# A modulation third taken off TensorE, its sums in halves, and the pieces loaded from GpSimd's queue

## The chip, the cores and the metric

The kernel runs on one core of a Trainium2 chip. The metric is the device time of one execution in microseconds. The profile shows the core's engines: PE is TensorE, DVE is VectorE, ACT is ScalarE, POOL is GpSimd, SP is SyncE, which here only issues DMA transfers.

## The reference

Two layers of a network over 256 latent and 256 context tokens of width 1024, in float32. Each layer is a token mixer (a long convolution, a gated linear recurrence called RG-LRU, a second recurrence called HGRN2, joined by gates: the merge) and an MLP, and each of the two is wrapped in norms that are scaled, shifted and gated by a modulation:

```python
for layer in range(DEPTH):
    ada_lat = silu(c) @ w_ada[layer] + b_ada[layer]          # 1024 -> 6 * 1024
    ada_ctx = silu(c_ctx) @ w_ada[layer] + b_ada[layer]
    sh1, sc1, g1, sh2, sc2, g2 = split(ada_lat, 6)            # the same for ctx
    u = rmsnorm(h, gains[0]) * (1 + sc1) + sh1
    m = mixer(u)
    h = h + g1 * rmsnorm(m, gains[1])
    f = square(relu((rmsnorm(h, gains[2]) * (1 + sc2) + sh2) @ w_mlp1[layer])) @ w_mlp2[layer]
    h = h + g2 * rmsnorm(f, gains[3])
```

Layer 1 needs no context output, so only its first two chunks (sh1, sc1) are needed for the context. The modulation is a product of two rows (latent and context) with a 1024 x 6144 matrix per layer: little arithmetic, 24 MB of weights. The long convolution also needs a filter per layer, a small network of sines.

## The kernel before

The program is unrolled, and a scheduler orders each engine's instructions by written order, priorities and readiness. The large products are split in high and low halves (three products for one). A weight unit of 1 MB arrives in one of two `raw` buffers, ScalarE writes its high half `wh`, VectorE subtracts to the low half `wl`, and TensorE uses both. A step of the loops below is one such unit, in most places 48 products of 512 columns.

Side work is written as generators and put into a queue `bg`; each loop step calls `bg.step()` once, which writes out the next piece of the first generator in the queue (a class `Pump`). The steps: one for each two column blocks of the projections (L1328), two for each gate branch of the merge beside its four gate steps (L1538), one for each of the 16 blocks of the first MLP product (L1648), one for each of 14 units of the second (L1660). At the end of layer 0's merge (L1540) and before layer 1's first norm (L1663) the queue is drained.

A third of a modulation, numbered s, is 2048 columns (two chunks) of one layer. The first third of layer 0 is computed at the start from a rearranged copy. The others are done in two ways:

- `ada_steps` (L382), for third 1 of layer 0: eight 1 MB pieces go through the `raw` buffers, and on each TensorE forms four narrow products (32 columns of weights `cst`, 512 columns of piece) that stand side by side in the array. Here and in `ada_sums` the two rows end in PSUM.
- `ada_sums` (L429), for the others: pieces of 128 x 512 arrive in four buffers `AM` by DMA from SP's queue, one transfer each, and VectorE multiplies each by a column of `cst` and adds it to a running sum `t` (one sum for each row and column block). A plan is four pieces; eight plans make a third. When a half is done (`both`, two rows) or a third (one row), four narrow products with a 0/1 column `sel` bring the sums over the partitions to PSUM. The first of them is tied behind the products that TensorE had at that step. The `AM` buffers hold the attention scores of the second recurrence at other times, and are zeroed on GpSimd afterwards.

`ada_out` copies the rows out, transposes them to columns (four transposes), adds the bias, and for thirds 1 and 2 multiplies the gate chunk by the norm's gains and stores it in DRAM, from where it is loaded as broadcast rows.

Order before: third 1 of layer 0 in the first projections of layer 0, third 2 of layer 0 for both rows in its merge, the three thirds of layer 1 in the MLP, then the filters of layer 1, in four groups, in the last steps of the second MLP product. The filters take their buffers from the 14 temporaries `t`, as do the sums.

In layer 1 the gates of the RG-LRU (`lru_gates`) are three products each, and those of the first channel block are tied behind 24 products that are written later (`tie(ins, 24)`).

Of the kernel before, what the change touches and what calls it, by code (L numbers as in the profile page):

```python
# [96 lines left out]
def prepare(inp):  # L97
# [11 lines left out]
    for w in range(2):  # L109
        for n in range(2):  # L110
            c = (w + 1) * 2048 + (2 * w + n) * 512
            for l in range(2):
                for r in range(2):
                    o = 32 * (2 * n + r) + w if (l, w) == (0, 1) else 32 * (2 * w + n) + r
# [12 lines left out]
    for l in range(2):  # L127
        for name, val in (("gain0", g["norm_gains"][l, 0]), ("gain2", g["norm_gains"][l, 2]), ("sw", g["hy_short_w"][l]),
# [3 lines left out]
            c = channel_cols(val)  # L132
# [30 lines left out]
def _body(ctx, tc, I, out, cfg):  # L163
# [100 lines left out]
    def add(o, a, b):  # L264
        tt(o, a, b, ALU.add)
# [67 lines left out]

    cst = kt([128, 8, 32])
    pool.memset(cst, 0.0)
    sel = kt([128, 2, 32])
    pool.memset(sel, 0.0)
    for r in range(2):
        pool.memset(sel[:, r, r:r + 1], 1.0)
    csg = kt([128, 8, 2])  # L340
    sigmoid()
    fn(csg, cc, AF.Sigmoid)
# [36 lines left out]
        mul(a0[:, ::-1, ks], part[:, :, 0], col(0, "gain0", 2 * qr, 2)[:, None, :].to_broadcast([128, 2, 2]))  # L379
        yield  # L380

    def ada_steps(l, s):  # L382
        acc = psx('a')
        for k in range(8):
            raw = raw_tile()
            dma(raw, I["w_ada"][l, k * 128:k * 128 + 128, s * 2048:s * 2048 + 2048])
            with tc.high_priority(cfg["AP"]):
                for j in range(4):
                    mm(acc[32 * j:32 * j + 32, :], cst[:, k, :], raw[:, j * 512:j * 512 + 512], k == 0, k == 7,
                       tile_position=(0, 32 * j))  # L390
            yield
        ada_out(l, s, acc, "(j r)")
        yield

    def ada_out(l, s, acc, order):

        rows = tmp()
        dve.tensor_copy(rows, acc)
        pt = psx('a')
        for b in range(4):  # L400
            pe.transpose(pt[:, b * 128:b * 128 + 128], rows[:, b * 128:b * 128 + 128], ident)
        cols = kt([128, 2, 2, 8], name="ac")
        if order == "(j r)":
            pv = pt.rearrange("p (b m n r) -> p r m n b", b=4, m=2, n=2)
        else:
            pv = pt.rearrange("p (b n r m) -> p r m n b", b=4, n=2, r=2)[:, :, :2]
        for r in range(2):
            for m in range(2):
                add(cols[:, r, m].rearrange("p (n b) -> p n b", b=4), pv[:, r, m],
                    col(l, "ba", 16 * s + 8 * m, 8).rearrange("p (n b) -> p n b", b=4))  # L410
        ada_cols[l, s] = cols
        if s > 0:
            w, j0 = s - 1, 2 * (s - 1)
            gr, br = tmp(), tmp()
            dma(gr, I["gate_rows"][l, w, :, 0])
            dma(br, I["gate_rows"][l, w, :, 1])
            add(rows, rows, br)
            mul(gr, gr, rows)
            st = dr.tile([2, 2, 512], F32, name=nm("gd"))
            for n in range(2):  # L420
                if order == "(j r)":
                    dma(st[:, n, :], gr[32 * (j0 + n):32 * (j0 + n) + 2, :])
                    continue
                for r in range(2):
                    o = 32 * (2 * n + r) + w
                    dma(st[r:r + 1, n, :], gr[o:o + 1, :])
            G_rows[l, w] = st

    def ada_sums(l, thirds):  # L429

        plans = [(s, both, i) for s, both in thirds for i in range(8)]

        def pieces(s, both, i):

            if not both:
                return [(i, s * 2048 + n * 512, n) for n in range(4)]
            half, kk = divmod(i, 4)
            return [(2 * kk + a, s * 2048 + half * 1024 + n * 512, n) for a in range(2) for n in range(2)]  # L440

        def load(q, plan):
            k, c, _ = pieces(*plan)[q]
            dma(AM[q], I["w_ada"][l, k * 128:k * 128 + 128, c:c + 512])

        def rows(acc, w, src, start, stop):
            for j, g in enumerate((3, 0, 1, 2)):
                after = last_mm[0]
                with tc.high_priority(cfg["AP"]):
                    ins = mm(acc[32 * g:32 * g + 32, :], w, src(g), start, stop, tile_position=(0, 32 * g))  # L450
                if j == 0:
                    tc.add_manual_dep(ins, after.name, no_sync, reason="behind the products of this step")

        for q in range(4):
            load(q, plans[0])
        acc, due = None, []
        for at_, (s, both, i) in enumerate(plans):
            yield
            while due:
                due.pop(0)()  # L460
            if i == 0 or (both and i == 4):
                sums = {}
            for q, (k, _, n) in enumerate(pieces(s, both, i)):
                for r in range(1 + both):
# [9 lines left out]
            def reduce(s=s, both=both, i=i, sums=sums):  # L474
                nonlocal acc
                if i == 3 or not both:
                    acc = psx('a')
                if both:
                    rows(acc, sel[:, i // 4, :], lambda g: sums[g % 2, g // 2], i == 3, i == 7)
                else:  # L480
                    rows(acc, sel[:, 0, :], lambda g: sums[0, g], True, True)
                if i == 7:
                    ada_out(l, s, acc, "(n r m)" if both else "(j r)")
            if i == 7 or (both and i == 3):
                due.append(reduce)
        yield
        while due:
            due.pop(0)()
        for a_t in AM:
            pool.memset(a_t, 0.0)  # L490
        yield

    def modulation(l, which):

        a, b = kt([128, 2, 8], name="ma"), kt([128, 2, 8], name="mb")
        gain = ("gain0", "gain2")[which]
        for r in range(2):
# [437 lines left out]
    def lru_gates(l, d, c, x, bd, sp_pos):  # L935
# [14 lines left out]
        for g, o in ((0, r), (1, i)):  # L950
            p = psx('l')
            cs = slice(c * 128, c * 128 + 128)
            if l == 1:
                ins = mm(p, bd[d][g][0][:, cs], hi, True, False)
                mm(p, bd[d][g][0][:, cs], lo, False, False)
                mm(p, bd[d][g][1][:, cs], hi, False, True)
                if c == 0:
                    tie(ins, 24)
            else:
                mm(p, bd[d][g][:, cs], xc, True, True)  # L960
            fn(o, p, AF.Sigmoid, bias=col(l, ("br", "bi")[g], d * 4 + c))
# [319 lines left out]
    def layer(l, S, xs=None, es=None):  # L1281
# [220 lines left out]
        for bi, b in enumerate(cfg["ORD"][l]):  # L1502
            Yb = ysplit(b)
            gates = raw_cols((GATES + b * 1024) // 128, 8, not full)
            if not gone:
                side.until("hg", done)
                sigmoid()
                gone = True
                if l == 0:
                    bg.put(ada_sums(0, ((2, True),)))  # L1510
            for x in gates:
                fn(x, x, AF.Sigmoid)
            if bi == 2:
# [112 lines left out]
        for r in range(0 if full else 2, 16):  # L1626
# [12 lines left out]
            for p in ps:  # L1639
# [206 lines left out]
```

## Time and profile before

| | us |
|---|---|
| median of 3 runs (1486.86 to 1488.83) | 1488.61 |
| the profiled execution | 1483.6 |
| its span | 1481.8 |
| TensorE busy in the span | 1454.7 |
| VectorE busy | 1072.9 |
| ScalarE busy | 745.6 |
| GpSimd busy | 25.3 |

The profile is of one execution; its span runs from the first to the last instruction. Matmuls are pipelined, so TensorE's busy time overlaps from one to the next, and the pace is read from start to start. Tiles are named without their numbers: `ra` is a 1 MB weight unit, `wh` and `wl` its halves, `b` and `t` are SBUF buffers and temporaries, `k` are kept tiles (the `AM` buffers, `cst`, `sel`, the identity), `pm` and `px` are PSUM. So `px<-ra,k` is a product of `ada_steps`, `t<-k,k,t` a sum of `ada_sums`, `px<-t,k` its reduction, `px<-k,t` a transpose, and each float32 product on narrow columns is recorded as two entries.

### The profile page before, as it was taken

How to read it: one execution, taken by the hardware profiler on the slowest of the kernel's cores; microseconds unless marked ns; L12 is line 12 of the kernel's file. 1: busy time of each engine (PE TensorE's matmuls, PEld its weight loads, DVE VectorE, ACT ScalarE, POOL GpSimd, SP SyncE). 2: the span in 40 equal slices, each digit the busy share in tenths (PEclk: the TensorE clock that was granted, in tenths of full speed). 3: DMA queues.
4: the chain of work that ended last, by engine and by line, in shares of the span. 5: the costliest groups of instructions: out<-in, count | busy, mean ns of one | idle time of the engine just before them, and what ended most of it. 6: DMA issues, size and time to landing. Idle time of an engine off the chain costs nothing.

```text
span 1481.8 us, 21719 instructions
## 1 busy us (share of the span) xinstructions
PE 1454.7 (98%) x8326; PEld 1222.8 (83%) x8326; DVE 1072.9 (72%) x1853; ACT 745.6 (50%) x1188; POOL 25.3 (2%) x245
## 2 busy tenths in 40 slices
PE   8999999999999999999999999999999999999998
PEld 4766878888888888888887877898889999899986
DVE  6676397978995277855747985776899886865544
ACT  6576555543242425543431223568877745565443
POOL 1000000000000000000000000000000000000000
PEclk9999999999999999999999999999999999999999
DMA  9554321232563242545846533132324345445553
GB/s 336 217 208 142 119 86 58 79 115 79 178 225 110 100 140 88 173 158 186 274 148 205 207 131 134 65 143 86 114 94 178 143 145 200 153 173 192 194 196 114
DMA packets 56999, 225.38 MB, mean 152 GB/s; under 512 B 6448, under 2 KB 8112, under 8 KB 37312
## 3 DMA queue, kind: packets, MB, share of 16 engines
q1 hardware_dynamic: 55168, 220.86, 42.4%
q10 hardware_dynamic: 1728, 3.15, 0.6%
q8 instruction: 65, 1.06, 0.3%
q14 instruction: 38, 0.31, 0.1%
HBM read 220.80 MB, written 3.18 MB: 151 GB/s over the span
## 4 chain that ended last, share of the span: by engine, by line
PE 80%; DVE 11%; ACT 5%; DMA 2%; issue 2%; SPq 0%; DVEq 0%; POOL 0%; ACTq 0%; POOLq 0%
PE pm L220 71%; PE px L220 9%; DVE b L220 5%; DVE t L220 3%; DVE wl L220 2%; ACT b L220 2%; ACT t L220 1%; DVE s L220 1%; ACT wh L220 1%; DMA k<-in_w_ada_dram 1%; DVE h L220 1%; ACT L220 1%; DMA h<-in_x_dram 0%; DMA ra<-in_w_in_dram 0%; DMA ra<-in_w_ada_dram 0%
## 5 line engine op out<-in xcount | busy, mean ns | idle before, releaser
L220 PE MATMUL pm<-b,wh 128*128 128x512 f32 (+1 forms) x3264 | 821.2, 342 | 1.8 <-DVE b L220 1.7
L220 PEld LDWEIGHTS pm<-b,wh 128*128 128x128 f32 x3264 | 562.9, 190 | 76.1 <-issue 3.5
L220 PE MATMUL pm<-b,wl 128*128 128x512 f32 (+1 forms) x1632 | 555.9, 341 | 0.0
L220 ACT ACTIVATE wh<-ra 128x1024 fp32r<-128x1024 f32 x278 | 293.5, 1059 | 496.9 <-PE pm L220 483.0
L220 DVE TENSOR_TENSOR wl<-ra,wh 128x1024 fp32r<-128x1024 f32 x278 | 338.6, 1223 | 241.6 <-ACT wh L220 237.2
L220 PEld LDWEIGHTS pm<-b,wl 128*128 128x128 f32 x1632 | 309.7, 190 | 35.0 <-issue 1.3
L220 PE MATMUL pm<-wh,b 128*128 128x512 f32 x976 | 304.2, 392 | 0.4 <-DVE b L220 0.4
L220 PEld LDWEIGHTS pm<-wh,b 128*128 128x128 f32 x976 | 182.6, 188 | 45.7 <-issue 3.6
L220 PE MATMUL pm<-wl,b 128*128 128x512 f32 x488 | 190.8, 391 | 0.0
L220 DVE TENSOR_TENSOR b<-b,b 128x512 fp32r<-128x512 f32 (+2 forms) x179 | 120.7, 682 | 29.7 <-PE pm L220 14.7
L220 DVE SCALAR_TENSOR_TENSOR t<-k,k,t 128x512 f32<-128x512 f32 x168 | 117.5, 748 | 15.1 <-DMA k<-in_w_ada_dram 14.7
L220 PEld LDWEIGHTS pm<-wl,b 128*128 128x128 f32 x488 | 91.6, 188 | 20.4 <-issue 1.6
L220 PE MATMUL pm<-b,b 128*128 128x256 f32 (+1 forms) x456 | 77.5, 324 | 2.3 <-DVE b L220 2.3
L220 ACT ACTIVATE t<-t 128x512 f32<-128x512 f32 (+3 forms) x124 | 60.9, 526 | 28.3 <-DVE t L220 27.2
L220 PEld LDWEIGHTS pm<-b,b 128*128 128x128 f32 x456 | 66.5, 190 | 10.0 <-DVE b L220 3.6
L220 ACT ACTIVATE b<-pm 128x512 f32<-128x512 f32 x88 | 50.5, 583 | 17.3 <-PE pm L220 9.2
L220 ACT ACTIVATE t<-pm 128x512 f32<-128x512 f32 (+1 forms) x74 | 42.4, 574 | 33.3 <-PE pm L220 30.8
L220 PE MATMUL px<-b,b 128*128 128x128 f32 (+1 forms) x280 | 55.8, 344 | 2.1 <-ACT b L220 1.3
L220 ACT ACTIVATE b<-b 128x512 f32<-128x512 f32 (+1 forms) x80 | 48.6, 627 | 11.4 <-DVE b L220 10.1
L220 ACT ACTIVATE b<-b,k 128x512 f32<-128x512 f32 x64 | 45.7, 739 | 8.3 <-DVE b L220 8.0
L220 PEld LDWEIGHTS px<-b,b 128*128 128x128 f32 x280 | 38.4, 191 | 12.6 <-issue 6.0
L220 ACT ACTIVATE t<-px 128x384 f32<-128x384 f32 (+3 forms) x50 | 21.9, 438 | 50.3 <-PE px L220 50.2
(114 smaller groups left out, 1062.1 us busy)
## 6 DMA issues: line engine op xcount, KB each, us to landing
ra<-in_w_mlp_dram SPq DMA_DIRECT2D x63, 1024.0 KB, 5.0
ra<-in_w_in_dram SPq DMA_DIRECT2D x58, 1024.0 KB, 4.8
k<-in_w_ada_dram SPq DMA_DIRECT2D x128, 256.0 KB, 3.6
ra<-in_w_proj_dram SPq DMA_DIRECT2D x12, 1024.0 KB, 4.8
b<-in_w_ada_first_dram SPq DMA_DIRECT2D x32, 256.0 KB, 5.3
ra<-in_w_ada_dram SPq DMA_DIRECT2D x8, 1024.0 KB, 5.8
ra<-in_w_out_dram SPq DMA_DIRECT2D x8, 1024.0 KB, 4.9
ra<-in_w_i_dram SPq DMA_DIRECT2D x4, 1024.0 KB, 4.8
```

The lines of the kernel that those rows point to most:

```text
L220: r = f(*a, **k)
```

## The change

- Third 1 of layer 0 is computed by `ada_sums`; `ada_steps` is gone.
- The work of `ada_sums` is a list of jobs (layer, third, half). A half has four plans and two rows, a job without a half has eight plans and the latent row. Every job ends in its own reduction and its own `ada_out`, which leaves out the transposes when the half is a gate and the gate part when it is not. In the merge of layer 0 there are now three half jobs (both halves of third 1, the first half of third 2), in the MLP the second half of third 2, then both halves of layer 1's third 0, then its thirds 1 and 2 for the latent row: 28 plans.
- The transfers of the pieces are issued from GpSimd's queue, not SP's.
- The filters of layer 1 have a queue of their own, `fg`, stepped at blocks 3, 6, 9, 12 and 15 of the first MLP product.
- The tie of layer 1's first gates is gone; the same three products are written by `three`.
- The kernel's arrays of gate gains and biases have their rows where the new order leaves them; for the transposes and sums of layer 1's thirds 1 and 2 the context row is left out.

```diff
-    def ada_steps(l, s):
-        acc = psx('a')
-        for k in range(8):
-            raw = raw_tile()
-            dma(raw, I["w_ada"][l, k * 128:k * 128 + 128, s * 2048:s * 2048 + 2048])
-            with tc.high_priority(cfg["AP"]):
-                for j in range(4):
-                    mm(acc[32 * j:32 * j + 32, :], cst[:, k, :], raw[:, j * 512:j * 512 + 512], k == 0, k == 7,
-                       tile_position=(0, 32 * j))
-            yield
-        ada_out(l, s, acc, "(j r)")
-        yield
-    def ada_out(l, s, acc, order):
+    def ada_out(l, s, acc, half):
         rows = tmp()
         dve.tensor_copy(rows, acc)
+        gate = s > 0 and half in (None, s - 1)
+        if half is None or not gate:
+            pt = psx('a')
+            for b in range(4):
+                pe.transpose(pt[:, b * 128:b * 128 + 128], rows[:, b * 128:b * 128 + 128], ident)
...
-    def ada_sums(l, thirds):
-        plans = [(s, both, i) for s, both in thirds for i in range(8)]
+    def ada_sums(jobs, zero):
+        plans = [(j, i) for j in jobs for i in range(8 if j[2] is None else 4)]
...
         def load(q, plan):
             k, c, _ = pieces(*plan)[q]
-            dma(AM[q], I["w_ada"][l, k * 128:k * 128 + 128, c:c + 512])
+            nc.gpsimd.dma_start(AM[q], I["w_ada"][plan[0][0], k * 128:k * 128 + 128, c:c + 512])
...
+            def reduce(job=job, sums=sums):
+                acc = psx('a')
+                for j, g in enumerate((3, 0, 1, 2)):
+                    src = sums[0, g] if job[2] is None else sums[g % 2, g // 2]
+                    after = last_mm[0]
+                    with tc.high_priority(cfg["AP"]):
+                        ins = mm(acc[32 * g:32 * g + 32, :], sel, src, True, True, tile_position=(0, 32 * g))
+                    if j == 0:
+                        tc.add_manual_dep(ins, after.name, no_sync, reason="behind the products of this step")
+                ada_out(job[0], job[1], acc, job[2])
+            if at_ + 1 == len(plans) or plans[at_ + 1][0] != job:
                 due.append(reduce)
         yield
         while due:
             due.pop(0)()
-        for a_t in AM:
-            pool.memset(a_t, 0.0)
+        if zero:
+            for a_t in AM:
+                pool.memset(a_t, 0.0)
...
             if l == 1:
-                ins = mm(p, bd[d][g][0][:, cs], hi, True, False)
-                mm(p, bd[d][g][0][:, cs], lo, False, False)
-                mm(p, bd[d][g][1][:, cs], hi, False, True)
-                if c == 0:
-                    tie(ins, 24)
+                three(p, bd[d][g][0][:, cs], bd[d][g][1][:, cs], hi, lo, True, True)
...
                 if l == 0:
-                    bg.put(ada_sums(0, ((2, True),)))
+                    bg.put(ada_sums(((0, 1, 0), (0, 1, 1), (0, 2, 0)), False))
...
         if full:
-            bg.put(ada_sums(1, ((0, True), (1, False), (2, False))))
-            bg.put(groups(filters(1), cfg["FG"]))
+            bg.put(ada_sums(((0, 2, 1), (1, 0, 0), (1, 0, 1), (1, 1, None), (1, 2, None)), True))
+            fg = Pump()
+            fg.put(groups(filters(1), cfg["FG"]))
...
             bg.step()
+            if full and r and r % 3 == 0:
+                fg.step()
...
             def start_next():
+                fg.drain()
                 bg.drain()
...
-    bg.put(ada_steps(0, 1))
```

## Rows read from the trace of the kernel before

**Rows 1.** Page, part 1: busy us, share of the span, instructions
```profile
PE 1454.7 (98%) x8326; PEld 1222.8 (83%) x8326; DVE 1072.9 (72%) x1853; ACT 745.6 (50%) x1188; POOL 25.3 (2%) x245
```

**Rows 2.** Page, part 4: shares of the chain that ended last
```profile
PE 80%; DVE 11%; ACT 5%; DMA 2%; issue 2%; SPq 0%; DVEq 0%; POOL 0%; ACTq 0%; POOLq 0%
```

**Rows 3.** The chain in order of time: start, us, what
```profile
496.76 82.33 PE pm L220 x363
```

**Rows 4.** Groups by line: count | busy, mean ns | idle before, releaser
```profile
L220 PE MATMUL px<-ra,k 128*32 128x512 f32 x64 | 8.3, 603 | 1.5 <-DMA ra<-in_w_ada_dram 1.5
...
L220 PE MATMUL px<-t,k 128*32 128x512 f32 x48 | 6.4, 604 | 0.0
```

**Rows 5.** Timeline of TensorE, one group of layer 0's second third: start, us, what
```profile
114.17 0.61 PE L220 MATMUL pm<-wh,b 128*128 128x512 f32 x2
114.71 1.06 PE L220 MATMUL px<-ra,k 128*32 128x512 f32 x8
115.71 0.50 PE L220 MATMUL pm<-wl,b 128*128 128x512 f32 x1
116.05 0.62 PE L220 MATMUL pm<-wh,b 128*128 128x512 f32 x2
```

**Rows 6.** Timeline of TensorE, a reduction and a set of transposes
```profile
448.24 1.07 PE L220 MATMUL px<-t,k 128*32 128x512 f32 x8
449.23 0.73 PE L220 MATMUL pm<-b,wh 128*128 128x512 f32 x2
...
496.17 0.60 PE L220 MATMUL px<-k,t 128*128 128x128 f32 x4
496.52 0.71 PE L220 MATMUL pm<-b,wh 128*128 128x512 f32 x2
```

**Rows 7.** Groups by line: sums of pieces, weight subtractions
```profile
L220 DVE TENSOR_TENSOR wl<-ra,wh 128x1024 fp32r<-128x1024 f32 x278 | 338.6, 1223 | 241.6 <-ACT wh L220 237.2 <-PE pm L220 1.2
...
L220 DVE SCALAR_TENSOR_TENSOR t<-k,k,t 128x512 f32<-128x512 f32 x168 | 117.5, 748 | 15.1 <-DMA k<-in_w_ada_dram 14.7
```

**Rows 8.** Waits of VectorE: us in total, times, longest
```profile
DVE t L220 <- DMA k<-in_w_ada_dram: 14.7, 14, 2.4
```

**Rows 9.** DMA issues: queue, count, KB each, median us to landing
```profile
k<-in_w_ada_dram SPq DMA_DIRECT2D x128, 256.0 KB, 3.6
...
b<-in_decay_dram SPq DMA_DIRECT2D x2, 256.0 KB, 6.8
```

**Rows 10.** Stretches: us, busy us (instructions) by engine, clock, DMA share, GB/s
```profile
150.00:175.00 25.00, 25.00 (x112) 20.69 (x111) 6.94 (x7) 11.18 (x16) 0.10 (x1) 1.00 0.30 105
448.00:493.00 45.00, 45.00 (x205) 36.14 (x203) 23.75 (x31) 13.09 (x17) 0.00 (x0) 1.00 0.29 105
601.00:652.00 51.00, 51.00 (x256) 43.35 (x254) 31.77 (x43) 21.66 (x32) 0.00 (x0) 1.00 0.55 186
831.00:919.00 88.00, 88.00 (x384) 69.06 (x383) 66.19 (x115) 21.81 (x30) 2.33 (x4) 1.00 0.40 142
```

**Rows 11.** Timeline of TensorE in the second MLP product
```profile
812.78 0.50 PE L220 MATMUL pm<-wh,b 128*128 128x512 f32 x1 [0.43 <-DVE b L220]
```

**Rows 12.** Timeline of GpSimd, at the start and in the merge
```profile
0.79 0.52 POOL L325 MEMSET k<- 128x512 f32 x1
...
437.76 0.53 POOL L490 MEMSET k<- 128x512 f32 x1 [73.78 <-DVE t L220]
```

**Rows 13.** Timeline of VectorE in layer 1, before the first gates
```profile
1000.69 0.69 DVE L220 TENSOR_TENSOR b<-b,b 128x512 fp32r<-128x512 f32 x1 [0.76 <-ACT b L220]
```

**Rows 14.** Timeline of TensorE in layer 1, the gates and later waits
```profile
1005.09 0.84 PE L220 MATMUL px<-b,b 128*128 128x512 f32 x3
...
1041.79 0.73 PE L220 MATMUL px<-b,b 128*128 128x512 f32 x2 [1.29 <-ACT b L220]
...
1100.18 0.94 PE L220 MATMUL px<-b,t 128*128 128x128 f32 x6 [1.95 <-ACT t L220]
```

**Rows 15.** Timeline of TensorE, layer 0's recurrences
```profile
211.25 0.94 PE L220 MATMUL px<-b,t 128*128 128x128 f32 x6 [2.57 <-ACT t L220]
```

More of the change, by code (lines that the diff above doesn't have):

```diff
@@ L112, in prepare @@
             for l in range(2):
-                for r in range(2):
-                    o = 32 * (2 * n + r) + w if (l, w) == (0, 1) else 32 * (2 * w + n) + r
+                for r in range(2 - l):
+                    o = 32 * (2 * n + r) if l == 0 else 32 * (2 * w + n)
                     rows[l, w, o] = g["norm_gains"][l, 1 + 2 * w, n * 512:n * 512 + 512]
@@ L335, in _body @@
     pool.memset(cst, 0.0)
-    sel = kt([128, 2, 32])
+    sel = kt([128, 32])
     pool.memset(sel, 0.0)
-    for r in range(2):
-        pool.memset(sel[:, r, r:r + 1], 1.0)
+    pool.memset(sel[:, 0:1], 1.0)
     csg = kt([128, 8, 2])
@@ L380, in ada_first @@
         yield
-    def ada_steps(l, s):
-        acc = psx('a')
-        for k in range(8):
-            raw = raw_tile()
-            dma(raw, I["w_ada"][l, k * 128:k * 128 + 128, s * 2048:s * 2048 + 2048])
-            with tc.high_priority(cfg["AP"]):
-                for j in range(4):
-                    mm(acc[32 * j:32 * j + 32, :], cst[:, k, :], raw[:, j * 512:j * 512 + 512], k == 0, k == 7,
-                       tile_position=(0, 32 * j))
-            yield
-        ada_out(l, s, acc, "(j r)")
-        yield
-    def ada_out(l, s, acc, order):
+    def ada_out(l, s, acc, half):
         rows = tmp()
         dve.tensor_copy(rows, acc)
[L399 to L413, printed above, removed]
+        gate = s > 0 and half in (None, s - 1)
[3 more added lines that the diff above has]
+                pe.transpose(pt[:, b * 128:b * 128 + 128], rows[:, b * 128:b * 128 + 128], ident)
+            if (l, s) not in ada_cols:
+                ada_cols[l, s] = kt([128, 2, 2, 8], name="ac")
+            cols = ada_cols[l, s]
+            for m in range(2) if half is None else (half,):
+                for r in range(1 if half is None else 2):
+                    if half is None:
+                        pv = pt.rearrange("p (b m n x) -> p x m n b", b=4, m=2, n=2)[:, 0, m]
+                    else:
+                        pv = pt.rearrange("p (b n r x) -> p x r n b", b=4, n=2, r=2)[:, 0, r]
+                    add(cols[:, r, m].rearrange("p (n b) -> p n b", b=4), pv,
+                        col(l, "ba", 16 * s + 8 * m, 8).rearrange("p (n b) -> p n b", b=4))
+        if gate:
+            w = s - 1
             gr, br = tmp(), tmp()
@@ L420, in ada_out, with pieces @@
             for n in range(2):
[L421 to L425, printed above, removed]
+                for r in range(2 if half is not None else 1):
+                    o = 32 * (2 * w + n) if half is None else 32 * (2 * n + r)
                     dma(st[r:r + 1, n, :], gr[o:o + 1, :])
             G_rows[l, w] = st
-    def ada_sums(l, thirds):
-        plans = [(s, both, i) for s, both in thirds for i in range(8)]
-        def pieces(s, both, i):
-            if not both:
+    def ada_sums(jobs, zero):
+        plans = [(j, i) for j in jobs for i in range(8 if j[2] is None else 4)]
+        def pieces(job, i):
+            l, s, half = job
+            if half is None:
                 return [(i, s * 2048 + n * 512, n) for n in range(4)]
-            half, kk = divmod(i, 4)
-            return [(2 * kk + a, s * 2048 + half * 1024 + n * 512, n) for a in range(2) for n in range(2)]
+            return [(2 * i + a, s * 2048 + half * 1024 + n * 512, n) for a in range(2) for n in range(2)]
         def load(q, plan):
             k, c, _ = pieces(*plan)[q]
-            dma(AM[q], I["w_ada"][l, k * 128:k * 128 + 128, c:c + 512])
[L446 to L452, printed above, removed]
+            nc.gpsimd.dma_start(AM[q], I["w_ada"][plan[0][0], k * 128:k * 128 + 128, c:c + 512])
         for q in range(4):
             load(q, plans[0])
-        acc, due = None, []
-        for at_, (s, both, i) in enumerate(plans):
+        due = []
+        for at_, (job, i) in enumerate(plans):
             yield
@@ L460, in ada_sums @@
                 due.pop(0)()
-            if i == 0 or (both and i == 4):
+            if i == 0:
                 sums = {}
-            for q, (k, _, n) in enumerate(pieces(s, both, i)):
-                for r in range(1 + both):
+            for q, (k, _, n) in enumerate(pieces(job, i)):
+                for r in range(1 if job[2] is None else 2):
                     c = cst[:, k, r:r + 1]
@@ L472, in ada_sums @@
                     load(q, plans[at_ + 1])
[L474 to L484, printed above, removed]
+            def reduce(job=job, sums=sums):
[9 more added lines that the diff above has]
+            if at_ + 1 == len(plans) or plans[at_ + 1][0] != job:
                 due.append(reduce)
@@ L496, in modulation @@
         gain = ("gain0", "gain2")[which]
-        for r in range(2):
+        for r in range(1 if (l, which) == (1, 1) else 2):
             sc = ada_cols[l, 0][:, r, 1] if which == 0 else ada_cols[l, 2][:, r, 0]
```

## The prediction

> **What bounds the kernel now.** I read the page's busy times first, then its chain, then the timeline of TensorE alone. TensorE is busy 98% of the span, VectorE 72%, GpSimd 2% [rows 1], and four fifths of the chain that ended last is TensorE's [rows 2]. Busy TensorE is not yet TensorE at its peak, so I looked at start-to-start times: in the densest stretch 363 products of 512 columns take 82.33 us, 0.2268 us each [rows 3]. That is the pace at which a removed product is worth its time, and the granted clock is 1.00 there and in the later stretches used below [rows 10], the higher of the two levels (2.4 GHz), so no part of the sum comes from the clock. A product of this kind therefore costs time wherever it stands, while VectorE, ScalarE and the queues cost only where TensorE is seen waiting for them. The question for each part is: does it take instructions off TensorE, or does it make TensorE wait?
>
> **1. The second third of layer 0 leaves TensorE.** Today it is eight groups of four narrow products, each group on one 1 MB piece; the trace records 64 entries, eight to a group [rows 4]. One group in a dense stretch: from the start at 114.17 to the start at 116.05, three ordinary products pass in 1.88 us where 3 x 0.227 = 0.68 would do, so the group costs 1.20 [rows 5]. From its own start to the next product's it is 1.00; some groups stand beside other fp32 products, where the neighbours lose less. I take 1.1 each: 8 x 1.1 = 8.8 us (ends 8.0 and 9.6). The groups also made TensorE wait 1.5 us for a piece [rows 4], which goes too. Together -10.3 us, ends -9.5 and -11.1. The four transposes and the gate rows of this third aren't removed; they move to the merge of layer 0. Its eight 1 MB transfers become 32 pieces of 256 KB there; the two `raw` buffers, which they shared with the weights, serve weights alone, for which I count nothing, as TensorE's only wait for a transfer of this loop is the 1.5 above.
>
> **2. What TensorE gets instead.** A finished sum is brought over the partitions by one group of four narrow products on a 0/1 column. Today there are 48 entries, six groups [rows 4]; afterwards there are eight jobs, so eight groups. One costs from 448.24 to 449.23, 0.99 us [rows 6], and its neighbours lose about 0.2 as in part 1: 2 x 1.2 = +2.4. Transposes: today five sets of four, afterwards six, since the two halves that are gates alone have none. A set takes 496.17 to 496.52, 0.35, with its neighbour 0.45 [rows 6]: +0.45.
>
> **3. More sums on VectorE.** Today 192 operations on pieces (24 of them first multiplications), afterwards 256: 56 more sums of 0.748 us and 8 more first multiplications of about 0.5 [rows 7], 46 us in all. I cost them at nothing, because of the cover. In layer 0's merge there are now three half jobs over 14 steps instead of two over ten. A step is 48 products, 48 x 0.2268 = 10.9 us, so a job has 4 x 10.9 + 1.2 = 44.7 us from one reduction to the next. Its 32 operations need 28 x 0.748 + 4 x 0.5 = 22.9 us, and the eight weight subtractions of four steps 8 x 1.223 = 9.8 [rows 7]: 32.7 of 44.7. The stretch into which the new jobs move, 448 to 493, has VectorE busy 23.8 of 45 the weight subtractions among them [rows 10]. In the MLP the first half job stands where a half job stands today (601 to 652, VectorE 31.8 of 51 [rows 10]); the last jobs move from 787-848 to about 830-919, where VectorE has 66.2 of 88 now, the last of the old sums and the filters among them [rows 10]; 32 x 0.748 = 23.9 more would make 90 of 88, but both of these move away. If the cover were gone, the weight subtractions behind a sum in VectorE's queue would be late and TensorE would wait for them, as it did for 0.43 us at 812.78, in the stretch where sums, splits and pieces now crowd together [rows 11]. The crowding there is relieved: -0.4 us (ends -0.4 and +5, a few such waits in each of the three crowded places).
>
> **4. Pieces from GpSimd's queue.** On SP a piece that waits for its buffer holds every weight load behind it. On GpSimd the pieces wait behind one another; GpSimd has no instruction at all in the stretches 448 to 493 and 601 to 652 [rows 10], and a piece's wait for the sum that frees its buffer holds only later pieces and the clearing of the four buffers, which is last. So SP's weight loads get a queue without these waits; today VectorE waits 14 times, 14.7 us, for a piece, 2.4 at the longest [rows 8]. The trace has no load from GpSimd. Below, I bound its landing by the same transfer from SP, 3.6 us, and above by the slowest 256 KB row of the list, 6.8 [rows 9]; I take 4.5, nearest the same transfer. A plan has 12 us / 4 = 3 us to spare, less some 3 us per job between a reduction and the next first sum: 2.2 us per plan. So up to 3.6 + 2.2 = 5.8 us nothing is late: 0. GpSimd also writes to SBUF while VectorE works: its 128x512 clearing took 0.53 us at 437.76 between sums and 0.52 at the idle start [rows 12], so I see no hold-up by sums. The Trainium skill has a rule against this edit: "SBUF — State Buffer", section "SBUF: two separate sides", says that a load issued from GpSimd can't have its descriptors written while VectorE runs a copy in its two-port mode, and gives 620 ns growing to 3100. By it a load would land an estimated 2.5 us later, 6.1 us, past the point above; the clearing shows no such hold beside the two-input sums, and no run so far shows a load.
>
> **5. Filters of layer 1 pumped apart.** The same instructions run at five places in the first MLP product instead of the last four steps of the second. TensorE pays the same there and here: 0. They hold six of the 14 temporaries for most of that time (rival c).
>
> **6. The tie of layer 1's first gates goes.** Their products now needn't stand behind 24 later ones, 24 x 0.2268 = 5.4 us. The first stands at 1005.09 [rows 14]; those of the second direction follow 2.7 us later, at 1007.8, and their input was written by 1000.69 + 0.69 = 1001.4 [rows 13]. 5.4 us earlier, at 1002.4, it would be just there. What could be won is bounded by TensorE's later waits for this chain, 1.29 us at 1041.79 and 1.95 at 1100.18 [rows 14]; lost could be one such wait for each direction, 2 x 1.29 = 2.6. I take -1.0 (ends -3.2, +2.6).
>
> **7. What is given back.** Everything behind the last of these groups comes about 10 us earlier. Where TensorE then waits for a recurrence it will wait longer if that chain doesn't move with it. Today that is 2.57 us at 211.25 [rows 15]. Between 150 and 175 VectorE is busy 6.9 of 25 us and ScalarE 11.2 [rows 10]: they have no backlog there and wait for projections, so the chain should move along. I take +1.0 (ends 0 and +10.3).
>
> **Sum.** -10.3 + 2.4 + 0.45 - 0.4 - 1.0 + 1.0 = -7.85 us. It is made against the profiled execution, 1483.6 us (span 1481.8 and 1.8 around it); the median of the runs is 5.0 above that, and the difference is taken off the median: 1488.61 - 7.85 = 1480.8 us.
>
> **Rivals.**
> a) The recurrences set the pace: the 10.3 us come back as longer waits at 211 and later. For it: VectorE is the chain's second engine [rows 2]. Against it: the idle stretch at 150-175. Time: 1480.8 + 9.3 = 1490.1.
> b) Slower: the pieces land late from GpSimd's queue. Place: the four half jobs that follow another job directly. Each microsecond of landing beyond 5.8 costs 4 us a job, as four plans stand in a row, 16 us in all, since TensorE stands at the reduction in its order. It decides from 5.8 + 7.85/16 = 6.3 us. At the slowest row, 6.8: 1480.8 + 16 = 1496.8. For it: the queue is new and VectorE is dense beside it; against it: the clearing at 437.76. The Trainium skill's rule of part 4 points this way; its 6.1 us would by this price give an estimated 1480.8 + 0.3 x 16 = 1485.6.
> c) Temporaries run out: six for the filters, four sums, three for gate rows leave one for the MLP's two activations. If these wait for the gate rows to be loaded, multiplied and stored, two transfers at the slowest 6.8 [rows 9] and two passes of 0.75 [rows 7] make 15.1 us; the two spare PSUM buffers cover one step, 10.9. It would cost 4.2: 1485.0. Against it: with 13 of 14 taken one is still free, and the two activations of a step need theirs one after the other.
> d) That the group isn't taken off TensorE can't be; the code has no product on raw pieces left.
>
> **Chances.** Forecast 0.61 (its own range 1474 to 1485), a 0.13, b 0.20, c 0.06. Under 0.2%, 3.0 us, a measurement of this kernel can't tell from no change. a lies within 3 us, b above, c on the edge, half and half: faster 0.64, same 0.16, slower 0.20. The range takes in a, c and the milder part of b, and 2 us below the forecast's own for part 6: 1472 to 1496.
>
> **What would show it.** Right: no px<-ra,k group, 64 px<-t,k entries, the time between 50 and 150 shorter by 10 us, 256 sums with waits for pieces near 1 us, TensorE dense from 375 to 780. Wrong: idle TensorE before px<-t,k (b), before px<-b,t at about 200 grown from 2.57 (a), ScalarE waiting for temporaries in the first MLP product (c), or px<-b,b near 1000 waiting for VectorE (part 6).

## The result, and the profile after

The changed kernel takes 1506.33 us (median of 4 runs, 1504.11 to 1509.04), the kernel before 1487.73 on the same chip: ratio 1.0134, 95% interval [1.0119, 1.0149]. It is slower by some 19 us where 7.9 less were forecast, and lies beyond the stated range (1472 to 1496).

Page, part 1, of the changed kernel: busy us, share of the span, instructions (answers [rows 1]). Then its part 4, the shares of the chain (answers [rows 2]).

```profile
PE 1461.2 (97%) x8282; PEld 1229.3 (82%) x8282; DVE 1111.5 (74%) x1910; ACT 744.6 (49%) x1188; POOL 113.2 (8%) x400
```
```profile
PE 60%; issue 15%; DVE 13%; ACT 6%; DMA 4%; POOL 1%; SPq 0%; DVEq 0%; POOLq 0%; ACTq 0%
```

TensorE has 44 instructions fewer and is still busy 6.5 us longer: some of its work ran at the lower clock. The chain now leaves TensorE more often, and the issues of the pieces (POOL) appear in it.

Groups by line (answers [rows 4] and [rows 7]), and who waited for whom (answers [rows 8]):

```profile
L220 DVE SCALAR_TENSOR_TENSOR t<-k,k,t 128x512 f32<-128x512 f32 x224 | 157.2, 745 | 30.4 <-DMA k<-in_w_ada_dram 30.3
...
L220 PE MATMUL px<-t,k 128*32 128x512 f32 x64 | 8.5, 605 | 0.0
```
```profile
DVE t L220 <- DMA k<-in_w_ada_dram: 30.3, 22, 4.3
...
PE pm L220 <- DVE b L220: 21.9, 13, 8.7
```

The second of these waits in the kernel before:

```profile
PE pm L220 <- DVE b L220: 4.4, 8, 1.5
```

There is no px<-ra,k group any more, the reductions are 64 entries that never waited, as forecast. But VectorE's wait for pieces has doubled, and TensorE waited 21.9 us for VectorE, once for 8.7.

To find the place, I set the start of the n-th ordinary product (counted from 0) in one trace against the same product in the other (both have 6816), in us:

```
product    before    after   later by
     100     60.69    64.78    +4.09   the start
     400    154.38   148.63    -5.75   behind the eight groups that went
    1400    439.08   433.08    -6.00
    1600    485.64   486.30    +0.66   merge of layer 0
    2400    653.11   658.85    +5.74   first MLP product
    2900    768.31   783.89   +15.58   (7.9 of it are filters, given back by 3600)
    3000    792.69   819.45   +26.76   second MLP product
    3600    940.97   964.41   +23.44
    6800   1471.14  1496.67   +25.52   low clock at 1067 and 1125
```

So the gain of 9.8 us came, and 29 went between 430 and 960. In that middle part TensorE's time divides as follows (us; products 1350 to 3700; start-to-start times of the records; 0.4 us or more over a product's own pace is counted as a stand; the rest of the 29 are transposes that moved here, 0.9):

```
                    before   after   SP's queue and merge repaired (below)
stands                1.4     21.7     5.5
products too slow     3.3      9.5     4.9
reductions            6.0      8.0     8.0
all                 532.7    562.1   541.3
```

The stretches of the changed kernel (us, busy us and instructions of PE, PEld, DVE, ACT and POOL, clock, DMA share, GB/s); the first and last answer [rows 10]:

```profile
448.00:493.00 45.00, 40.32 (x171) 32.65 (x170) 39.82 (x59) 10.78 (x13) 8.59 (x16) 0.96 0.54 181
...
783.00:798.00 15.00, 6.27 (x19) 4.63 (x17) 8.91 (x13) 1.06 (x1) 5.05 (x9) 0.66 0.83 288
831.00:919.00 88.00, 84.88 (x370) 67.66 (x369) 73.13 (x125) 18.59 (x23) 18.86 (x32) 0.98 0.51 178
```

And three stands of TensorE in the timeline, the two of the merge and the longest of all (start, us, what, idle before and its releaser):

```profile
458.60 0.74 PE L220 MATMUL pm<-b,wh 128*128 128x512 f32 x2 [1.46 <-DVE b L220]
...
470.30 0.77 PE L220 MATMUL pm<-b,wh 128*128 128x512 f32 x1 [3.21 <-DVE b L220]
...
793.00 0.79 PE L220 MATMUL pm<-wh,b 128*128 128x512 f32 x1 [8.73 <-DVE b L220]
```

None stands at a reduction. (Where a stand is given start to start, over the product's own pace, it is some 0.2 us longer than the idle time shown here: 1.6, 3.4 and 8.9.) Around the long stand the clock was at the lower level: granted 0.66 in the mean of 783 to 798, where the kernel before has 1.00 in its second MLP product, from 831 to 919 [rows 10].

**Why VectorE was late at 793.** Its timeline:

```profile
783.82 0.75 DVE L220 SCALAR_TENSOR_TENSOR t<-k,k,t 128x512 f32<-128x512 f32 x1 [2.76 <-DMA k<-in_w_ada_dram]
785.79 1.42 DVE L220 SCALAR_TENSOR_TENSOR t<-k,k,t 128x512 f32<-128x512 f32 x2 [1.22 <-DMA k<-in_w_ada_dram]
787.37 0.75 DVE L220 SCALAR_TENSOR_TENSOR t<-k,k,t 128x512 f32<-128x512 f32 x1 [0.17 <-DMA k<-in_w_ada_dram]
788.34 0.75 DVE L220 SCALAR_TENSOR_TENSOR t<-k,k,t 128x512 f32<-128x512 f32 x1 [0.22 <-DMA k<-in_w_ada_dram]
789.01 1.22 DVE L220 TENSOR_TENSOR wl<-ra,wh 128x1024 fp32r<-128x1024 f32 x1
790.14 1.41 DVE L220 SCALAR_TENSOR_TENSOR t<-k,k,t 128x512 f32<-128x512 f32 x2
791.86 0.75 DVE L220 SCALAR_TENSOR_TENSOR t<-k,k,t 128x512 f32<-128x512 f32 x1 [0.31 <-DMA k<-in_w_ada_dram]
792.53 0.42 DVE L220 CAST b<-b 128x512 fp32r<-128x512 f32 x1
```

The CAST at 792.53 is the split that the product at 793.00 needs. It is 0.42 us of work, and stood in VectorE's queue behind eight sums. VectorE waited for a piece five times among them, 4.7 us in all.

**Why it was late at 458 and 470.** VectorE again, in the merge:

```profile
410.57 1.23 DVE L220 TENSOR_TENSOR wl<-ra,wh 128x1024 fp32r<-128x1024 f32 x1 [1.34 <-ACT wh L220]
416.01 1.23 DVE L220 TENSOR_TENSOR wl<-ra,wh 128x1024 fp32r<-128x1024 f32 x1 [4.21 <-ACT wh L220]
...
445.29 0.68 DVE L220 COPY t<-px 128x512 f32<-128x512 f32 x1
...
448.36 0.48 DVE L220 TENSOR_SCALAR t<-k,k 128x512 f32<-128x512 f32 x1
```

From 410 to 443 it does six weight subtractions and idles 4.21 us between two of them. The second job's first multiplication (448.36) comes only behind the COPY that takes the first job's reduced rows, which needs TensorE's reduction at 442. Then the job's operations fall together with the merge's own: 39.8 of 45 us from 448 to 493, where the kernel before has 23.8 [rows 10]. In the kernel before the second job's sums ran ahead into the idle stretch, and VectorE was busy 31.17 of 33 us there:

```profile
410.00:443.00 33.00, 33.00 (x148) 27.32 (x147) 31.17 (x46) 13.39 (x19) 1.70 (x4) 1.00 0.67 219
```

In the changed kernel TensorE waits for PSUM buffers that VectorE empties late. Ahead of the stand at 470:

```profile
463.70 4.72 DVE L220 SCALAR_TENSOR_TENSOR t<-k,k,t 128x512 f32<-128x512 f32 x7
468.34 1.22 DVE L220 TENSOR_TENSOR wl<-ra,wh 128x1024 fp32r<-128x1024 f32 x1
469.48 1.28 DVE L220 TENSOR_TENSOR b<-pm,b 128x512 f32<-128x512 f32 x2
```

Seven sums stand between VectorE's emptying of the bank (b<-pm,b, at 469.48) and its last such operation before, at 460.27.

### The profile page after: what moved, and what is told of

It is laid out like the page before. It is cut to its first block, busy times and chain, and to the rows that moved or that the text cites. A ratio compares the mean times of both kernels' runs of the same rounds, so it can differ in the third digit from the quotient of the medians.

```text
span 1507.3 us, 21764 instructions
## 1 busy us (share of the span) xinstructions
PE 1461.2 (97%) x8282; PEld 1229.3 (82%) x8282; DVE 1111.5 (74%) x1910; ACT 744.6 (49%) x1188; POOL 113.2 (8%) x400
## 4 chain that ended last, share of the span: by engine, by line
PE 60%; issue 15%; DVE 13%; ACT 6%; DMA 4%; POOL 1%; SPq 0%; DVEq 0%; POOLq 0%; ACTq 0%
PE pm L220 52%; PE px L220 8%; DVE b L220 5%; DVE t L220 5%; DMA k<-in_w_ada_dram 4%; DVE wl L220 2%; ACT b L220 2%; ACT t L220 2%; ACT wh L220 1%; POOL k L430 1%; DVE s L220 1%; ACT L220 1%; DVE h L220 0%; DMA b<-in_w_ada_first_dram 0%; ACT s L220 0%
## 5 line engine op out<-in xcount | busy, mean ns | idle before, releaser
L220 DVE SCALAR_TENSOR_TENSOR t<-k,k,t 128x512 f32<-128x512 f32 x224 | 157.2, 745 | 30.4 <-DMA k<-in_w_ada_dram 30.3
L430 POOL DMA_DIRECT2D k<-in_w_ada_dram x160 | 90.4, 565 | 467.1 <-DVE t L220 458.7
L220 ACT ACTIVATE t<-t 128x512 f32<-128x512 f32 (+3 forms) x124 | 60.7, 526 | 25.5 <-DVE t L220 24.4
L220 ACT ACTIVATE t<-pm 128x512 f32<-128x512 f32 (+1 forms) x74 | 42.4, 575 | 36.8 <-PE pm L220 32.7
L220 ACT ACTIVATE b<-pm 128x512 f32<-128x512 f32 x88 | 50.5, 583 | 12.8 <-PE pm L220 4.8
L190 POOL MEMSET t<- 128x1 f32 x146 | 13.5, 104 | 477.5 <-DVE b L220 182.3
```

Source lines behind the costliest of these rows:

```text
L190: nc.gpsimd.memset(x[:, 0:1], 0.0)
L220: r = f(*a, **k)
L430: nc.gpsimd.dma_start(AM[q], I["w_ada"][plan[0][0], k * 128:k * 128 + 128, c:c + 512])
```

## The experiments

Two theories stood against each other. **Q**: GpSimd's queue brings the pieces later. **O**: the order in which VectorE was given its work is at fault, whatever the queue. All times in us; the ratio is to the kernel before on the same chip, and the differences below are taken from the ratios, since not all of them ran on the same chip. A ratio is good to 0.10 to 0.23%, so a difference of two is good to some 2 to 4 us. The waits are those of the one profiled execution.

| kernel | median | ratio, 95% interval | VectorE waited for pieces |
|---|---|---|---|
| changed | 1506.3 | 1.0134 [1.0119, 1.0149] | 30.3 |
| a_sp | 1492.5 | 1.0049 [1.0032, 1.0065] | 13.9 |
| a_late | 1498.1 | 1.0082 [1.0060, 1.0105] | 29.9 |
| a_fg | 1517.9 | 1.0216 [1.0193, 1.0239] | 29.6 |
| b_pool | 1490.5 | 1.0034 [1.0021, 1.0048] | 31.4 |
| a_ml_sp | 1484.9 | 1.0000 [0.9988, 1.0011] | 13.7 |
| a_ml_sp_tie | 1485.2 | 0.9996 [0.9986, 1.0007] | 11.5 |
| a_late_sp | 1484.4 | 0.9989 [0.9979, 0.9998] | 13.3 |
| b_fg | 1489.3 | 1.0021 [1.0011, 1.0030] | 10.9 |
| a_noload | 1487.3 | 1.0007 [0.9995, 1.0018] | none |
| a_ml_pri | 1501.5 | 1.0106 [1.0087, 1.0125] | 32.6 |
| a_ml_sp_pri | 1484.6 | 0.9995 [0.9983, 1.0006] | 12.8 |
| a_late_sp_pri | 1483.0 | 0.9980 [0.9967, 0.9993] | 9.4 |

**a_sp: the changed kernel, pieces from SP's queue.**

```
-            nc.gpsimd.dma_start(AM[q], I["w_ada"][...])
+            dma(AM[q], I["w_ada"][...])
```

> The changed kernel with one part undone: the pieces are loaded from SP's queue again. Theory Q (the new queue is what costs: each piece is issued in 0.54 us one behind another and lands late, and the splits behind the waiting sums come late): the 8.9 us stand of TensorE at 784 and the 1.5 at 798 go, with the slow clock behind them, about 13 us: 1493, and VectorE's wait for pieces falls from 30 to about 15 us. Theory O (the order in which VectorE was given its work costs, whatever the queue; the landing is 3.5 us from GpSimd against 3.6 from SP): the stand in the merge at 457 to 470 stays at about 5 us, the ones in the second MLP product change by a few us either way: 1500 to 1510.

Measured 1492.5: 0.85% less than the changed kernel, 12.6 us. Q is right about the second MLP product (26.76 later at the 3000th product became 12.6), O about the merge, whose two stands stay. The queues side by side; first GpSimd's, in the changed kernel (duration of an issue min/median/max in ns; time to landing in us):

```profile
L430 POOL DMA_DIRECT2D k<-in_w_ada_dram x160: 536/538/823, 281.1 to 905.8; - x160
...
DMA to landing us min/median/max: 2.8/3.5/8.1
```

and SP's, in a_sp:

```profile
L430 SPq DMA_DIRECT2D k<-in_w_ada_dram x160: 327/328/1091, 278.8 to 898.6; - x160
...
DMA to landing us min/median/max: 2.5/3.5/6.2
```

The second view rests on 21 of the 160 transfers. The records of all 160 arrivals give a median of 3.5, a mean of 4.0 and a longest of 8.1 us from GpSimd, and 3.3, 3.8 and 6.5 from SP: the landing is hardly later. What differs more is the way to the issue. One round from GpSimd's queue (VectorE's and GpSimd's timelines of the changed kernel):

```profile
764.99 2.08 DVE L220 SCALAR_TENSOR_TENSOR t<-k,k,t 128x512 f32<-128x512 f32 x3 [4.31 <-DMA k<-in_w_ada_dram]
...
769.17 1.41 DVE L220 SCALAR_TENSOR_TENSOR t<-k,k,t 128x512 f32<-128x512 f32 x2 [0.31 <-DMA k<-in_w_ada_dram]
```
```profile
766.04 1.86 POOL L430 DMA_DIRECT2D k<-in_w_ada_dram  x3 [4.34 <-DVE t L220]
```

and from SP's (a_sp):

```profile
760.98 2.73 DVE L220 SCALAR_TENSOR_TENSOR t<-k,k,t 128x512 f32<-128x512 f32 x4
764.46 1.52 DVE L220 SCALAR_TENSOR_TENSOR t<-k,k,t 128x512 f32<-128x512 f32 x2 [0.74 <-DMA k<-in_w_ada_dram]
```
```profile
761.76 3.81 SPq L430 DMA_DIRECT2D k<-in_w_ada_dram  x5
```

A sum takes 0.75, so the first buffer was free at 765.74 and 761.73. GpSimd issued 0.30 later, SP 0.03; the next sum on that buffer began 3.43 later by GpSimd, 2.73 by SP. Over the 60 pieces issued from 750 to 960, the records give 4.65 us in the mean from the last sum on a buffer to the landing of its next piece, nine in ten within 6.94, and from SP's queue 4.32 and 6.17. With four buffers the 4.65 us are 1.16 us a piece, and the sums of the last jobs read a piece once, in 0.67 us start to start: there a longer round is soon waited for.

One issue stands out. The buffer of the 114th piece was free at 777.07, at the end of the first of these sums, and its issue began only at 779.95 (the changed kernel):

```profile
776.33 1.41 DVE L220 SCALAR_TENSOR_TENSOR t<-k,k,t 128x512 f32<-128x512 f32 x2
```
```profile
779.95 1.60 POOL L430 DMA_DIRECT2D k<-in_w_ada_dram  x3 [3.42 <-DVE b L220]
```

That is 2.88 us instead of 0.3, and the two issues behind it began 2.75 and 1.69 us after theirs were free. These pieces, with the 113th, which landed 8.0 us after its issue, are behind the first three of the five waits ahead of 793 (2.76, 1.22 and 0.17 us). In all five kernels that load from GpSimd's queue the 114th issue began 2.88 us after its buffer was free, whatever VectorE did at that time; no record here tells what held it. So part of the queue's price is one late row of pieces at a bad place, and how much was not taken apart. The wait is not slower work: a sum takes 745 ns in the changed kernel, 746 in a_sp and 748 in the kernel before.

**a_late: a job's reduction written behind the next plan's sums.**

```
             yield
-            while due:
-                due.pop(0)()
             if i == 0: ...
             (the plan's sums)
+            while due:
+                due.pop(0)()
```

> The changed kernel with one thing moved: a job's reduction and the finishing of its rows are written behind the next plan's sums, no longer ahead of them. Theory O: in the merge of layer 0 VectorE does the second job's sums from 410 on, where it idles 4 of every 5.4 us, and not after 448, so TensorE's stands of 1.6 and 3.4 us at 457 and 467 go with the 3.4 us of half clock behind them: 6.6 us less up to 490; in the MLP the sums come earlier too, which may go either way: 1495 to 1500. Theory Q: the merge has no wait for a piece above 1 us, so nothing of its loss is due to order, and the time stays at 1503 to 1509.

Measured 1498.1, 0.52% or 7.7 us less: O is right about the merge, which by the two traces (products 1400 to 1600) accounts for 6.7 of them. VectorE now does the second job's sums in the stretch where it idled (its timeline in a_late):

```profile
416.44 3.40 DVE L220 SCALAR_TENSOR_TENSOR t<-k,k,t 128x512 f32<-128x512 f32 x5 [2.01 <-DMA k<-in_w_ada_dram]
...
420.90 4.72 DVE L220 SCALAR_TENSOR_TENSOR t<-k,k,t 128x512 f32<-128x512 f32 x7
```

and of the stretch 410 to 443 it is busy 26.5 us; first a_late, then the changed kernel:

```profile
410.00:443.00 33.00, 33.00 (x150) 26.39 (x149) 26.48 (x38) 13.07 (x18) 7.12 (x14) 1.00 0.63 213
```
```profile
410.00:443.00 33.00, 33.00 (x151) 26.58 (x149) 7.69 (x7) 13.44 (x19) 0.06 (x1) 1.00 0.30 104
```

Both stands of the merge are gone; the long one of the second MLP product is still there with 5.4 us.

**a_fg: the changed kernel, filters behind the sums again.**

```
-            fg = Pump()
-            fg.put(groups(filters(1), cfg["FG"]))
+            bg.put(groups(filters(1), cfg["FG"]))
```

> The changed kernel with one part undone: the filters of layer 1 are pumped behind the sums again, in the last steps of the second MLP product. Theory F (the filters pumped apart hold temporaries and VectorE in the first MLP product and push the sums into the second): the stand of 8.9 us at 784 goes, 1490 to 1495. Theory O: the sums stay where they are, the stand at 642 (1.3 us) goes and one at the end of the second product may come: 1502 to 1509.

Measured 1517.9, 0.8% more: a miss for both. The stand at 784 stayed, so F is out, but the filters are now last in a longer row and TensorE waits for them at the end of the second product:

```profile
977.52 0.45 PE L220 MATMUL px<-k,t 128*128 128x128 f32 x1 [4.07 <-ACT s L220]
...
983.17 2.18 PE L220 MATMUL px<-k,t 128*128 128x128 f32 x9 [5.21 <-DVE t L220]
```

With one more job in the row, and on GpSimd's queue, pumping the filters apart is needed.

**b_pool: the kernel before, pieces from GpSimd's queue, nothing else.**

> The kernel before with one part of the change alone: the pieces are loaded from GpSimd's queue. Theory Q: VectorE's wait for pieces grows from 14.7 to 25 us or more and TensorE stands for splits in the MLP: 1495 to 1502. Theory O: within 3 us of the kernel before: 1485 to 1491.

Measured 1490.5, 5 us more than the kernel before on the same chip: at the upper end of O's times, but more than its 3 us, and below Q's times. Q's doubled wait came (14.7 to 31.4, as in the changed kernel), its price did not: 5 us here and 12.6 there, where the order differs and 32 more pieces are loaded. The length of the wait alone does not set its price. TensorE waited 7.7 us for VectorE here, 21.9 in the changed kernel:

```profile
DVE t L220 <- DMA k<-in_w_ada_dram: 31.4, 18, 5.1
...
PE pm L220 <- DVE b L220: 7.7, 9, 1.7
```

**a_ml_sp: both repairs** (SP's queue; reduction behind the next sums in the merge alone).

> The changed kernel with two repairs: pieces from SP's queue again (which alone took 14 us off), and in the merge of layer 0 alone the reduction and its rows written behind the next plan's sums. If the two losses are separate (order in the merge, queue in the MLP): 1492.5 minus the 6.6 us of the merge, 1486. If VectorE's sums in the merge only push their cost on, to the stretch behind it: 1491 to 1493.

Measured 1484.9, the time of the kernel before: the two losses are separate and add up, 12.6 + 7.7 against 19.9 together (1.0134 to 1.0000).

**a_ml_sp_tie: and the tie put back.**

> The same as the version with the two repairs, and the tie of layer 1's first gates put back. If taking the tie away cost TensorE's waits of 2.0, 1.5 and 0.6 us beyond the 950 mark (the delay against the kernel before grows by 2.1 us behind 1000): 2 us below the version with the two repairs. If these waits come from the earlier stages' shift: the same within 1 us.

Measured 1485.2: no difference that can be seen. The difference of the two is good to some 2 us, so the tie is worth less than that here.

**a_late_sp: SP's queue, and all reductions behind the next sums.**

> As the version with the two repairs, but the reductions of the MLP's jobs are written behind the next sums too. On GpSimd's queue this lost about 2 us in the first MLP product and 9 at the start of the second, and gave 4 back at its end. If those losses were order: 2 to 6 us above the version with the two repairs. If they were GpSimd's queue: the same within 2 us.

Measured 1484.4: the same within 2 us. So what a_late lost in the MLP was the queue's. In the MLP the later writing of the reductions gains nothing either.

**b_fg: the kernel before, filters pumped apart alone.**

> The kernel before with one part of the change alone: the filters of layer 1 pumped apart, in five steps of the first MLP product. Taking this part out of the changed kernel cost 11.6 us, as the longer row of sums there pushes the filters to the end of the second product, where TensorE stands 10 us for them. In the kernel before the row of sums is shorter and the filters still fit behind it: within 3 us of the kernel before, 1483 to 1488. If moving them is a gain by itself: 1478 to 1482; if they are in VectorE's way in the first product: 1488 to 1492.

Measured 1489.3, 2 to 4 us more: a miss for the 1483 to 1488, and inside the range for filters in VectorE's way. By itself the part is no gain. TensorE's longest wait for VectorE ahead of the filters' narrow products is 3.2 us there.

**a_noload: the changed kernel without the pieces' transfers.**

```
-                if at_ + 1 < len(plans):
-                    load(q, plans[at_ + 1])
```

> The changed kernel without the loads of the pieces behind the first four (it leaves these transfers out, so all sums are made of the same four pieces); everything else of its order stays. Theory Q: the splits come late only because the sums ahead of them wait for pieces, so the stands of 8.9, 1.5, 2.8 and 0.8 us at 784 to 897 and the half clock behind them go, about 19 us, and the two in the merge stay: 1486 to 1490. If it were VectorE's mere work (64 more operations) that makes the splits late, the stands stay: above 1500.

Measured 1487.3. The same operations of VectorE, without a wait for a piece: the second MLP product stands no more (a_noload, then the changed kernel),

```profile
764.00:799.00 35.00, 35.00 (x154) 28.40 (x153) 31.34 (x53) 8.61 (x10) 0.00 (x0) 1.00 0.37 127
```
```profile
764.00:799.00 35.00, 25.62 (x103) 20.36 (x101) 23.27 (x34) 8.77 (x13) 11.72 (x21) 0.85 0.78 261
```

with VectorE busier than before, 31.3 of 35 us. So neither the added operations nor a full VectorE cost TensorE anything there; the waits inside its queue did. This version takes the transfers' traffic away together with the waits (DMA share 0.37 instead of 0.78), but traffic alone is not the cause: a_sp has a share of 0.85 in the same stretch, and TensorE is busy 32.75 us of it. The stands of the merge are still there (1.4 and 3.2 us idle).

**a_ml_pri: GpSimd's queue kept, merge repaired, splits of the second product at higher priority.**

```
-                split(hi, lo, hb[kk])
+                with tc.high_priority(400):
+                    split(hi, lo, hb[kk])
```

> The changed kernel with GpSimd's queue kept, the merge repaired, and the splits of the second MLP product given a higher priority, as the weights' have. If a better place of the splits in VectorE's order can stand in for a faster queue: 1488 to 1492 (1498 without it). If the sums that wait still stand ahead of the splits that are due: 1496 to 1500.

Measured 1501.5, above both ranges: no help. (The 1498 is a_late's time; a kernel with the merge repaired and nothing else was not run.) The stand is still there, 9.25 us up to 785.15, and the CAST that ends it, at 784.68, again stands behind eight sums with four waits for pieces. Why the priority did not move it ahead of them was not tested.

**a_ml_sp_pri and a_late_sp_pri: the same priority on top of the repaired versions.**

> The version with the two repairs (SP's queue, merge) and the higher priority for the splits. It stood 2.0, 1.0 and 1.1 us at 771, 775 and 874 for splits; if the priority puts them ahead of waiting sums: 1481 to 1483, faster than both kernels. If not: 1484 to 1486.

> As the version with SP's queue and all reductions behind the next sums (1484.4, the lowest so far, 0.1% under the kernel before), with the higher priority for the splits. It stood 3.3 and 1.2 us at 773 and 778 with 6.8 us of half clock behind them. If the priority takes these away: 1478 to 1481; if not: 1483 to 1486.

Measured 1484.6 and 1483.0. The first is what was expected without an effect. The second is faster than both kernels, by 0.2% of the one before (0.9980 [0.9967, 0.9993]), less than hoped, and not clearly faster than a_late_sp (0.9989). Page, part 1, of a_late_sp_pri:

```profile
PE 1450.5 (98%) x8282; PEld 1223.2 (83%) x8282; DVE 1111.8 (75%) x1910; ACT 744.5 (50%) x1188; POOL 23.0 (2%) x240
```

## Why the prediction was wrong

The terms read from TensorE's own rows held. Two terms set at nothing failed, more sums on VectorE (part 3) and the pieces from GpSimd's queue (part 4); both let TensorE wait for VectorE.

1. **The eight groups leave TensorE**: forecast -10.3, measured -9.8 between the 100th and the 400th product.
2. **Reductions and transposes**: forecast +2.4 and +0.45; the table has +2.0 for the reductions, and one set of transposes more was recorded.
3. **More sums, at nothing: failed in the merge.** The step counted 32.7 us of work in 44.7 between two reductions, and quoted 23.8 us busy of 45 for the stretch the job moves into [rows 10]. The 32.7 leave out the merge's own work, which those 23.8 us hold. Added, as it should have been, 23.8 + 22.9 is 46.7 of 45. The job would have fitted only by running ahead into the idle time before 443, as in the kernel before; the new order put its first operation behind the reduced rows of the job before. Cost 7.7 us (a_late).
4. **GpSimd's queue, at nothing up to a landing of 5.8: failed.** The landing was not the fault (3.5 in the median, 4.0 in the mean, 4.5 taken). The point of 5.8 was worked out for the reductions alone, the last of four plans, and with the 3 us to spare of part 3. What stands behind a waiting instruction was worked out for SP's weight loads, and for VectorE's sums only in part 3, as an end of +5 us; part 4 did not join it to the waits for pieces. Behind them stand splits and weight subtractions for the very next product. Cost 12.6 us (a_sp); without waits for pieces TensorE has no stand in the MLP (a_noload).
5. **Filters, at nothing**: +2 to 4 alone (b_fg), and needed together with the longer row of sums (a_fg, 12 us).
6. **The tie**, -1.0: nothing to be seen, inside its ends. The first gates' products, at 1025 in the changed kernel, waited for nothing.
7. **Given back**, +1.0: the wait of 2.57 [rows 15] grew by 0.7.

```profile
205.93 0.94 PE L220 MATMUL px<-b,t 128*128 128x128 f32 x6 [3.27 <-ACT t L220]
```

Rival b had the right queue and sign, but neither the place (no reduction was waited for) nor the cause (the median landing is far below 5.8); that its 16 us are near the 12.6 is luck. Rivals a and c did not come: that wait is all of a, and ScalarE's wait for VectorE's temporaries fell from 27.2 to 24.4. With both losses repaired the time is that of the kernel before, and not 7.9 below: what is left in the middle part are 4 us of stands more than before, the reductions, and some slow products behind the stands, and in that trace another 2.3 us at the lower clock near 1100, which a_late_sp's trace does not have.

The 4 us that the profiled run lost in the first 60 us are no part of the change. TensorE's instructions are the same in all the kernels up to there, and the 100th product comes between 0.2 us earlier and 4.1 us later than in the kernel before, with none to 10.2 us at the lower clock. Open is what held GpSimd's 114th issue, and what makes some landings late.

## What to carry to other kernels

An engine's idle share pays for new work only where its queue has the idle time: find out behind which instruction the new one will stand, add the stage's own work to it, and ask what stands behind each instruction that waits. A wait on an engine off the critical path is priced by what is queued behind it, so a wait doubled alike cost 5 us in one order and 13 in another. When work is cut into jobs, and the engine idles before the next one, write the finishing of one behind the start of the next: that took 7.7 us off the merge here, and nothing off the MLP.

## What the hardware showed that I had not expected

- A load issued by GpSimd keeps it for 0.54 us (SP 0.33) and begins 0.30 us after its buffer is free (SP 0.03); it lands nearly as soon in the median (3.5 against 3.3), with a longer tail (8.1 against 6.5).
- The 114th of these issues began 2.88 us after its buffer was free, in each of the five kernels that load from GpSimd's queue, with 128 pieces or 160.
- 17 of the 160 issues took 0.76 to 0.82 us, each beside a CAST of VectorE or two TENSOR_SCALARs: 0.22 more. From issue to landing these took 3.7 us in the median and the others 3.4; of the 29 over 5 us, 2 are among them. The Trainium skill, "SBUF — State Buffer", section "SBUF: two separate sides", tells of GpSimd shut out while VectorE copies in its two-port mode, 620 ns growing to 3100. The trace shows a hold of 0.22 us beside such operations, and not that size; nor does it make the late landings, of which 27 of 29 had an ordinary issue. The 114th issue is late by about that size, but at the same count in five kernels, and in the changed one beside no copy.
- Up to the last products the clock was at the lower level (1.2 instead of 2.4 GHz) for 37.5 us in all in the changed kernel's trace and 3.4 in the kernel before's: 10.2 us in the first 30, 10.2 from 787.3, inside and behind the long stand, and 3.4 each at or just behind TensorE's waits of 3.27, 3.21, 2.67, 1.29 and 1.95 us. Such waits also passed without it: 3.22 in a_noload at 463, and the same 1.29 and 1.95 in the kernel before. Products slowed by it made up 6.2 of the 29 us.
